# The first head's queries and keys projected together while x arrives, its values around the rows' norm

## The chip, the cores and the metric

The kernel runs on one core of a Trainium2 chip. A core has a matrix engine (TensorE, "PE" in the profile; its weight loads are "PEld"), three engines that work on tiles (VectorE "DVE", ScalarE "ACT", GpSimd "POOL"), and SyncE "SP", which here issues all transfers; sixteen DMA engines carry them. Each engine runs its own list of instructions in order and waits on semaphores for the others. The metric is the device time of one execution in microseconds; less is better.

## The reference

One layer of a streaming encoder is computed for 16 meta tokens, a prompt of 512 frames and 64 frames of a running stream, in fp32. Cut to what matters here:

```python
h = rmsnorm(x, norm_attn_g)              # x: (L, 2048)
z = h @ w_in                             # (2048, 3904): q | k | v of 8 heads, 128 columns each,
                                         # then latent queries, latent keys/values, rotary key
qd, kd, vd = z[..., :1024], z[..., 1024:2048], z[..., 2048:3072]
s = qd . kd * DIFF_SCALE + rel_bias[t5_bucket(kpos - qpos)]     # per head, two halves of 64
p = softmax(s[0]) - lam * softmax(s[1])
o_d = rmsnorm(p @ vd, diff_subln_g) * (1 - lam_init)
# a second head group on the latents, output projection, residual, SwiGLU FFN, final norm
```

`rmsnorm` divides each row by the root of its mean square. The new keys and values of each head are outputs too.

## The kernel before, in words

All 592 tokens (64 sample, 16 meta, 512 prompt) are held transposed: D = 2048 lies in 16 slices of 128 partitions (`KC` = 16), tokens along the free dimension, in two halves of 296 (`TH`). For accuracy each fp32 operand is split into a high and a low part (`split`, L155 to L157: ACT makes the high part at L156, DVE the low part at L153), and a product is three matmuls, high by high, high by low, low by high (`mm3`), for each half of the tokens: six matmuls for a slice. A projection (`project`) of 128 output columns takes 16 slices; its weights come in two halves of 8 slices (`weights`), each one transfer of 512 KB, split in one piece.

*The start.* x is loaded token by token into tiles `xn`, six row tiles (`tok`) for each quarter of D (`load_x`). `transpose_x` turns one slice into PSUM (L112) and has ACT and DVE write `xh` and `xl`, scaled by the norm's gain (`split_scaled`, L160 and L161), and DVE copy the slice to `xt` (L377, L382), which is stored to DRAM as `xspill` for the residual. Even slices use one pair of PSUM banks (`pxt`), odd slices two single ones (`pxa`, `pxb`). When the last slice of a quarter has been transposed, ACT squares its six row tiles with a running sum (L387) into `ssp`, and, since `xn` has two buffers per row tile, the quarter after next is loaded. The projection of head 0's queries runs along: slice kc is projected while slice kc + 1 is transposed.

The division by the norm is put off: `xh` and `xl` carry no norm, and the projected rows are multiplied by `rb`, the reciprocal root of each token's mean square in all partitions. It is made after the 16 slices: `ss` (L426, L427), `rsqrt`, six products with the identity (`prb`, L108 through the helper) and a copy (L434). Then comes the relative bias: `ptr` is the product of the bias table with a one-hot matrix, copied to `trs` (L446), stored to DRAM, spread over 128 rows (`tsk`, L449) and read back skewed as `bias` by each head.

*After the start* a planner (`Streams`) writes out the order of PE's work: `projections` goes through the heads (queries, keys, values, and then the latents), and each head's attention (`diff_attend`) takes PE between its slices, by rank. The planner counts PE's time and gives PSUM banks back after fixed delays (`st.give`). PE's instructions stay in the order in which the program names them; on the other engines the instructions are put in order when the program is built, by when their operands are expected.

PSUM has eight banks: two pairs for projections (`pjt`), one pair `sp` for scores and `pxt`, one single bank `tp`, one single bank `po`.

Of the kernel before, what the change touches and what calls it, by code (L numbers as in the profile page):

```python
# [19 lines left out]
P = 128  # L20
D = 2048
KC = D // P
# [93 lines left out]
def encoder_step(  # L116
# [19 lines left out]
    def load(dst, src):  # L136
        nc.sync.dma_start(dst, src)
# [155 lines left out]
    def ev(ps, n=TH):  # L293
        return ps[:, :, 0:n]
# [19 lines left out]
    with ExitStack() as ph:  # L314
# [7 lines left out]
        def pjt():  # L322
            return pj.tile([P, 2, 512], F32, name="ps", tag="ps")
# [4 lines left out]
        def tbank(name="tp"):  # L328
            return pst.tile([P, 512], F32, name=name, tag="tp")
# [11 lines left out]


        tok = [(0, OWN), (OWN, P), (208, 88), (TH, P), (424, P), (552, 40)]
        ps0 = pjt()
        with tc.tile_pool(name="xn", bufs=1) as xn:
            ssp = az.tile([P, 6, 4], F32, name="ssp")
            V.memset(ssp, 1.0)
            junk = xn.tile([P, 512], F32, name="junk")
            xt_in = {}

            def load_x(cg):
                cs = slice(cg * 512, (cg + 1) * 512)
                for j, (o, n) in enumerate(tok):
                    t = xn.tile([P, 512], F32, name="xn", tag=f"xn{j}", bufs=2)
                    if j == 0:
                        load(t[0:NS, :], x_sample[:, cs])
                        load(t[NS:OWN, :], meta[:, cs])
                    else:
                        load(t[0:n, :], x_prompt[o - OWN:o - OWN + n, cs])
                    xt_in[cg, j] = t  # L360

            def transpose_x(kc):
                cg, k = kc // 4, kc % 4
                if kc % 2 == 0:
                    sp = sbig("pxt")
                    banks = [sp[:, 0, 0:TH], sp[:, 1, 0:TH]]
                else:
                    banks = [tbank("pxa")[:, 0:TH], pso.tile([P, 512], F32, name="pxb", tag="po")[:, 0:TH]]
                for j, (o, n) in enumerate(tok):
                    b = o // TH  # L370
                    PE.transpose(banks[b][:, o - b * TH:o - b * TH + n],
                                 xt_in[cg, j][0:n, k * P:(k + 1) * P], ident[0:n, 0:n])
                xt = ztile("xt")
                g = gA[:, kc:kc + 1]
                if kc % 2 == 0:
                    split_scaled(hv(xh[kc]), hv(xl[kc]), ev(sp), g)
                    V.tensor_copy(hv(xt), ev(sp))  # L377
                else:
                    for b in range(2):
                        c = slice(b * TH, (b + 1) * TH)  # L380
                        split_scaled(xh[kc][:, c], xl[kc][:, c], banks[b], g)
                        V.tensor_copy(xt[:, c], banks[b])  # L382
                for o, n, c in KEPT:
                    store(xspill[kc, :, c:c + n], xt[:, o:o + n])
                if k == 3:
                    for j, (o, n) in enumerate(tok):
                        S.activation(junk[0:n], xt_in[cg, j][0:n], AF.Square, accum_out=ssp[0:n, j, cg:cg + 1])  # L387
                    if cg + 2 < 4:
                        load_x(cg + 2)

            load_x(0)
            gains = xn.tile([P, P], F32, name="gains")
            V.memset(gains, 0.0)
            rows = 0
            for g in (g_attn, g_ffn, g_fin, g_q, g_kv, g_sub):
                n = g.shape[0] // P
                load(gains[rows:rows + n, :], g.rearrange("(c p) -> c p", p=P))
                rows += n
            load_x(1)
            pg = tbank("pg")  # L400
            PE.transpose(pg[:, 0:P], gains, ident)
            gT = cp.tile([P, rows], F32, name="gT")
            V.tensor_copy(gT, pg[:, 0:rows])
            gA, gF, gE, gq, gkv, g08 = (gT[:, a:b] for a, b in ((0, 16), (16, 32), (32, 48), (48, 52), (52, 54), (54, 55)))
            first = project(ps0, w_in[:, 0:P], xs1)
            transpose_x(0)
            for kc in range(KC):
                if kc + 1 < KC:
                    transpose_x(kc + 1)
                next(first)  # L410

        ap = ph.enter_context(tc.tile_pool(name="ap", bufs=1))
# [13 lines left out]
        V.reduce_sum(ss, ssp, axis=AX.X)  # L426
        V.tensor_scalar(ss, ss, 1.0 / D, EPS, op0=ALU.mult, op1=ALU.add)  # L427
        rsqrt(rc, ss)
        pb = sbig("prb")
        for j, (o, n) in enumerate(tok):  # L430
            b = o // TH
            PE.matmul(pb[:, b, o - b * TH:o - b * TH + n], rc[0:n, j:j + 1].to_broadcast([n, P]),
                      ident[0:n, 0:n], start=True, stop=True)
        V.tensor_copy(hv(rb), ev(pb))  # L434

        with tc.tile_pool(name="xc", bufs=1, side="right") as xc:

            oh = xc.tile([32, NREL], F32, name="oh")
            load(oh, c_onehot)
            rbt = xc.tile([32, H], F32, name="rbt")  # L440
            load(rbt, rel_bias)
            ptr = sbig("ptr")
            trs = xc.tile([H, NREL], F32, name="trs")
            for i, (a, b) in enumerate(((0, 512), (512, NREL))):
                PE.matmul(ptr[0:H, i, 0:b - a], rbt, oh[:, a:b], start=True, stop=True)
                V.tensor_copy(trs[:, a:b], ptr[0:H, i, 0:b - a])  # L446
            store(trow, trs)
            for h in range(H):
                nc.sync.dma_start(tsk[h], trow[h:h + 1, :].to_broadcast([P, NREL]))  # L449

            lamt = xc.tile([P, 4, DH], F32, name="lamt")
            load(lamt, lam_p.rearrange("a b -> (a b)").unsqueeze(0).to_broadcast([P, 4 * DH]).rearrange(
                "p (a b) -> p a b", a=4))
            lprod = xc.tile([P, 2, DH], F32, name="lprod")
            lsum = xc.tile([P, 2], F32, name="lsum")
            V.tensor_tensor(lprod, lamt[:, 0:4:2, :], lamt[:, 1:4:2, :], op=ALU.mult)
            V.reduce_sum(lsum, lprod, axis=AX.X)
            S.activation(lsum, lsum, AF.Exp)
            V.memset(lamv[:, 0:1], 1.0)
            V.tensor_tensor(lamv[:, 1:2], lsum[:, 0:1], lsum[:, 1:2], op=ALU.subtract)  # L460
            V.tensor_scalar(lamv[:, 1:2], lamv[:, 1:2], LAM_INIT, None, op0=ALU.add)
            V.tensor_scalar(g08, g08, 1.0 - LAM_INIT, None, op0=ALU.mult)
# [113 lines left out]

        def projections():
            for h in range(H):
                ps = ps0 if h == 0 else pjt()
                if h:  # L580
                    yield from project(ps, w_in[:, h * P:(h + 1) * P], xs1)
                if h >= 2:
                    yield [scored[h - 2]]
                z = ztile()
                V.scalar_tensor_tensor(hv(z), ev(ps), DH ** -0.5, hv(rb), op0=ALU.mult, op1=ALU.mult)
                for c in range(2):
                    r = slice(c * DH, (c + 1) * DH)
                    split(qs[h % 2][c][0][r, :], qs[h % 2][c][1][r, :], z[r, :])

                ps = pjt()  # L590
                yield from project(ps, w_in[:, OFF_K + h * P:OFF_K + (h + 1) * P], xs1)
                if h >= 1:
                    yield [nat[2 * h - 1], nat[2 * h - 2]]
                z = ztile()
                V.tensor_tensor(hv(z), ev(ps), hv(rb), op=ALU.mult)
                kh = ap.tile([P, TP], F32R, name="kh", bufs=2)
                kl = ap.tile([P, TP], F32R, name="kl", bufs=2)
                split(kh[:, 0:T], kl[:, 0:T], z)
                nat[2 * h] = st.spawn(0, keys(h, z, kh, kl))

                ps = pjt()
                yield from project(ps, w_in[:, OFF_V + h * P:OFF_V + (h + 1) * P], xs1)
                if h >= 2:
                    yield [att[h - 2]]
                z = ztile()
                V.tensor_tensor(hv(z), ev(ps), hv(rb), op=ALU.mult)
                vh = ap.tile([P, 6, P], F32R, name="vh", bufs=2)
                vl = ap.tile([P, 6, P], F32R, name="vl", bufs=2)
                nat[2 * h + 1] = st.spawn(0, values(h, z, vh, vl))
                att[h] = st.spawn(1, diff_attend(h, kh, kl, vh, vl),  # L610
                                  [nat[2 * h], nat[2 * h + 1]] + ([att[h - 1]] if h else []))
# [5 lines left out]
                zs[i] = zl.tile([P, T], F32, name=f"zl{i}")  # L617
                V.tensor_tensor(hv(zs[i]), ev(ps), hv(rb), op=ALU.mult)

        for name in ("sp", "tp", "po"):  # L620
            st.bank(name, 1)
        st.spawn(9, projections())
        st.run()

# [794 lines left out]
```

## Time and profile before

| | |
|---|---|
| time, median of 3 runs | 2583.15 us (2583.13 to 2589.03) |
| the profiled execution's own time | 2593.06 us |
| its span in the profile | 2590.9 us |
| mean granted TensorE clock | 0.983 |
| PE busy | 2464.9 us, 95% |
| DVE, ACT, POOL busy | 71%, 41%, 29% |
| DMA | 307.73 MB, mean 119 GB/s |

The profile is of one execution. A page gives busy times, a picture of the span in 40 slices, the costliest groups of instructions with the idle time before them and what ended it. A row of the timeline has start, duration, engine, line, operation, written tile <- read tiles, and in brackets the idle time before it with its releaser. A row of the waits has who waited for whom: total, times, longest. A row of the windows has the stretch and its length, then busy time of PE, PEld, DVE, ACT, POOL with instruction counts, granted clock, DMA share, GB/s.

### The profile page before, as it was taken

To read this page: it belongs to the slowest core of one execution; us is meant where nothing else is said; L and a number is where in the kernel's file an instruction comes from. 1 tells how busy PE (TensorE), PEld (TensorE's weight loads), DVE (VectorE), ACT (ScalarE), POOL (GpSimd) and SP (SyncE) were. 2 spreads that over 40 slices of the span, in tenths; PEclk is the share of its full clock that TensorE was granted. 3 is DMA by queue.
4 is the path that set the end of the run, shared out by engine and by line. 5 is a ranking of instruction groups with operands and counts; after the bars stand their busy time and mean duration, and the time that the engine had idled before them with its cause. 6 is when DMAs were issued, how large, how long until landed. Compare 5 with 4: busy or idle time off the path is not lost. (4 is left out here: it accounts for less than half of the span.)

```text
span 2590.9 us, 44881 instructions
## 1 busy us (share of the span) xinstructions
PE 2464.9 (95%) x17847; PEld 2399.3 (93%) x17847; DVE 1837.4 (71%) x2955; ACT 1056.5 (41%) x1879; POOL 763.5 (29%) x614
## 2 busy tenths in 40 slices
PE   6999999989999999999999999999999899999997
PEld 5999999988999888999999999999999899999996
DVE  5455555556565568777677787777778899899874
ACT  5234333334443444333333333333334344444444
POOL 0000000000000265545545455464543221221244
PEclk9999999999999899999999999999999899999998
DMA  6433233334331553333333333333335543443334
GB/s 197 126 93 93 80 86 86 81 104 121 99 99 58 170 152 124 106 113 121 130 116 108 111 122 128 116 128 108 109 126 177 189 146 98 146 146 101 98 107 130
DMA packets 330563, 307.73 MB, mean 119 GB/s; under 512 B 24707, under 2 KB 298506, under 8 KB 330354
## 3 DMA queue, kind: packets, MB, share of 16 engines
q1 hardware_dynamic: 330354, 304.87, 37.7%
q8 instruction: 140, 2.29, 0.4%
q14 instruction: 69, 0.57, 0.1%
HBM read 250.82 MB, written 56.68 MB: 119 GB/s over the span
## 5 line engine op out<-in xcount | busy, mean ns | idle before, releaser
L1051 PE MATMUL m<-bh,wh 128*128 128x288 f32 x3584 | 971.8, 296 | 8.3 <-ACT wh L156 6.3
L1051 PE MATMUL m<-bl,wh 128*128 128x288 f32 x3584 | 970.4, 295 | 0.0
L1051 PEld LDWEIGHTS m<-bh,wh 128*128 128x128 f32 x3584 | 676.3, 189 | 10.7 <-ACT wh L156 8.2
L1051 PEld LDWEIGHTS m<-bl,wh 128*128 128x128 f32 x3584 | 680.0, 190 | 0.1
L1055 PE MATMUL m<-bh,wl 128*128 128x288 f32 x3584 | 589.3, 300 | 38.1 <-DVE wl L153 35.9
L1020 POOL TENSOR_TENSOR ws<-raw 128x512 f32<-128x512 f32 x256 | 359.3, 1412 | 765.1 <-DVE wl L153 533.6
L1055 PEld LDWEIGHTS m<-bh,wl 128*128 128x128 f32 x3584 | 512.2, 189 | 57.1 <-DVE wl L153 56.4
L156 ACT ACTIVATE wh<-ws 128x512 fp32r<-128x512 f32 (+1 forms) x340 | 288.3, 848 | 475.9 <-PE m L1051 339.2
L153 DVE TENSOR_TENSOR wl<-ws,wh 128x512 fp32r<-128x512 f32 (+1 forms) x340 | 377.5, 1115 | 56.7 <-ACT wh L156 52.7
L153 DVE TENSOR_TENSOR wl<-raw,wh 128x512 fp32r<-128x512 f32 x416 | 401.2, 985 | 14.3 <-ACT wh L156 14.1
L156 ACT ACTIVATE wh<-raw 128x512 fp32r<-128x512 f32 x416 | 248.0, 625 | 339.6 <-PE m L1051 297.6
L108 PE MATMUL ps<-xh,wh 128*128 128x296 f32 x992 | 228.9, 312 | 6.9 <-ACT wh L156 6.9
L108 PE MATMUL ps<-xl,wh 128*128 128x296 f32 x992 | 218.3, 302 | 0.0
L108 PE MATMUL ps<-xh,wl 128*128 128x296 f32 x992 | 218.1, 301 | 0.0
L108 PEld LDWEIGHTS ps<-xh,wh 128*128 128x128 f32 x992 | 163.1, 192 | 11.1 <-ACT wh L156 7.0
L108 PEld LDWEIGHTS ps<-xl,wh 128*128 128x128 f32 x992 | 163.5, 191 | 0.0
L108 PEld LDWEIGHTS ps<-xh,wl 128*128 128x128 f32 x992 | 163.1, 191 | 0.3 <-DVE wl L153 0.3
L1020 DVE TENSOR_TENSOR ws<-ws,raw 128x512 f32<-128x512 f32 x128 | 94.0, 737 | 97.6 <-POOL ws L1020 92.5
L153 DVE TENSOR_TENSOR wl<-wr,wh 128x1024 fp32r<-128x1024 f32 (+1 forms) x110 | 117.7, 1070 | 45.3 <-ACT wh L156 36.4
L1272 DVE TENSOR_TENSOR y<-y,m 128x288 f32<-128x288 f32 x280 | 125.4, 448 | 21.5 <-PE m L1055 20.3
L156 ACT ACTIVATE wh<-wr 128x1024 fp32r<-128x1024 f32 (+1 forms) x110 | 101.8, 929 | 80.5 <-PE ps L108 72.2
L518 POOL MEMSET bias<- 64x64 f32 x8 | 1.4, 170 | 409.7 <-DMA bias<-tsk 247.8
(361 smaller groups left out, 3426.7 us busy)
## 6 DMA issues: line engine op xcount, KB each, us to landing
raw<-in_ffn_w_gate SPq DMA_DIRECT2D x44, 1024.0 KB, 7.7
raw<-in_ffn_w_up SPq DMA_DIRECT2D x44, 1024.0 KB, 6.3
raw<-in_ffn_w_down SPq DMA_DIRECT2D x40, 1024.0 KB, 5.4
wr<-in_w_in SPq DMA_DIRECT2D x60, 512.0 KB, 4.0
actspill<-c SPq DMA_DIRECT2D x44, 288.0 KB, 2.2
sumspill<-c SPq DMA_DIRECT2D x20, 576.0 KB, 3.0
bl<-sumspill SPq DMA_DIRECT2D x80, 144.0 KB, 3.4
bl<-actspill SPq DMA_DIRECT2D x68, 144.0 KB, 4.1
```

Of the source, the lines that this page charges most:

```text
L108: self.tc.keep_in_program_order(self.pe.matmul(out, lhsT, rhs, start=start, stop=stop))
L153: V.tensor_tensor(lo, src, f32(hi), op=ALU.subtract)
L156: S.activation(hi, src, AF.Copy)
L518: G.memset(bias[0:64, 464:528], -BIG)
L1020: engine.tensor_tensor(w[:, k:k + m, :], pick(xs), pick(ys), op=op)
L1051: PE.matmul(banks[p], wh[:, k, :], x, start=first and new and k == 0 and x is hi, stop=False, skip_group_check=not new)
L1055: PE.matmul(banks[p], wl[:, k, :], hi, start=False, stop=last and k == n - 1, skip_group_check=not new)
L1272: V.tensor_tensor(c, c, banks[p], op=ALU.add)
```

## The change

- x's row tiles have four buffers, so no load of x waits for a transposition; the loads of the gains move ahead of x, and those of the first weights stand between the quarters of x.
- Head 0's queries and keys are projected in the same loop, slice by slice, into the two pairs of banks of `pjt`; the keys' weights have buffers of their own in the pool `xn` (`first_weights`).
- Head 0's values are projected after that loop into the pair `sp` (`psv`): the first 8 slices before the norm's products `prb`, the other 8 after them. `prb` and `ptr` move to the single banks; `ptr`'s two pieces use the one bank `tp` in turn.
- In `projections`, head 0 only takes the finished banks; the planner starts with the bank `sp` taken and gets it back when the values are read.

```diff
-        ps0 = pjt()
+        psq, psk, psv = pjt(), pjt(), None
         with tc.tile_pool(name="xn", bufs=1) as xn:
+            gains = xn.tile([P, P], F32, name="gains")
+            V.memset(gains, 0.0)
+            rows = 0
+            for g in (g_attn, g_ffn, g_fin, g_q, g_kv, g_sub):
+                n = g.shape[0] // P
+                load(gains[rows:rows + n, :], g.rearrange("(c p) -> c p", p=P))
+                rows += n
...
-                    t = xn.tile([P, 512], F32, name="xn", tag=f"xn{j}", bufs=2)
+                    t = xn.tile([P, 512], F32, name="xn", tag=f"xn{j}", bufs=4)
...
                         S.activation(junk[0:n], xt_in[cg, j][0:n], AF.Square, accum_out=ssp[0:n, j, cg:cg + 1])
-                    if cg + 2 < 4:
-                        load_x(cg + 2)
+
+            def first_weights(hf):
+
+                r = slice(hf * 8 * P, (hf + 1) * 8 * P)
+                return [weights(w_in[r, c:c + P].rearrange("(k p) c -> p k c", p=P), 8, P, pool=pool)
+                        for c, pool in ((0, wp), (OFF_K, xn))]
 
             load_x(0)
-            gains = xn.tile([P, P], F32, name="gains")
...
+            ws = first_weights(0)
             load_x(1)
+            load_x(2)
+            ws = [ws, first_weights(1)]
+            load_x(3)
...
-            first = project(ps0, w_in[:, 0:P], xs1)
             transpose_x(0)
             for kc in range(KC):
                 if kc + 1 < KC:
                     transpose_x(kc + 1)
+                for ps, (wh, wl) in zip((psq, psk), ws[kc // 8]):
+                    mm3([ps[:, 0, 0:TH], ps[:, 1, 0:TH]], wh[:, kc % 8, :], wl[:, kc % 8, :],
+                        halves(xh[kc]), halves(xl[kc]), kc == 0, kc == KC - 1)
+            psv = sbig("psv")
+            first = project(psv, w_in[:, OFF_V:OFF_V + P], xs1)
+            for _ in range(8):
                 next(first)
...
-        pb = sbig("prb")
+        pb = [tbank("prb"), pso.tile([P, 512], F32, name="prb", tag="po")]
         for j, (o, n) in enumerate(tok):
             b = o // TH
-            PE.matmul(pb[:, b, o - b * TH:o - b * TH + n], rc[0:n, j:j + 1].to_broadcast([n, P]),
+            PE.matmul(pb[b][:, o - b * TH:o - b * TH + n], rc[0:n, j:j + 1].to_broadcast([n, P]),
                       ident[0:n, 0:n], start=True, stop=True)
-        V.tensor_copy(hv(rb), ev(pb))
+        for b in range(2):
+            V.tensor_copy(rb[:, b * TH:(b + 1) * TH], pb[b][:, 0:TH])
+        for _ in first:
+            pass
...
-            ptr = sbig("ptr")
             trs = xc.tile([H, NREL], F32, name="trs")
-            for i, (a, b) in enumerate(((0, 512), (512, NREL))):
-                PE.matmul(ptr[0:H, i, 0:b - a], rbt, oh[:, a:b], start=True, stop=True)
-                V.tensor_copy(trs[:, a:b], ptr[0:H, i, 0:b - a])
+            for a, b in ((0, 512), (512, NREL)):
+                ptr = tbank("ptr")
+                PE.matmul(ptr[0:H, 0:b - a], rbt, oh[:, a:b], start=True, stop=True)
+                V.tensor_copy(trs[:, a:b], ptr[0:H, 0:b - a])
...
-                ps = ps0 if h == 0 else pjt()
+                ps = psq if h == 0 else pjt()
...
-                ps = pjt()
-                yield from project(ps, w_in[:, OFF_K + h * P:OFF_K + (h + 1) * P], xs1)
+                ps = pjt() if h else psk
+                if h:
+                    yield from project(ps, w_in[:, OFF_K + h * P:OFF_K + (h + 1) * P], xs1)
...
-                ps = pjt()
-                yield from project(ps, w_in[:, OFF_V + h * P:OFF_V + (h + 1) * P], xs1)
+                ps = pjt() if h else psv
+                if h:
+                    yield from project(ps, w_in[:, OFF_V + h * P:OFF_V + (h + 1) * P], xs1)
...
                 V.tensor_tensor(hv(z), ev(ps), hv(rb), op=ALU.mult)
+                if h == 0:
+                    st.give("sp", 1.5)
...
-        for name in ("sp", "tp", "po"):
-            st.bank(name, 1)
+        for name, n in (("sp", 0), ("tp", 1), ("po", 1)):
+            st.bank(name, n)
```

More of the change, by code (lines that the diff above doesn't have):

```diff
@@ L387, in transpose_x @@
                         S.activation(junk[0:n], xt_in[cg, j][0:n], AF.Square, accum_out=ssp[0:n, j, cg:cg + 1])
-                    if cg + 2 < 4:
-                        load_x(cg + 2)
+            def first_weights(hf):
+                r = slice(hf * 8 * P, (hf + 1) * 8 * P)
+                return [weights(w_in[r, c:c + P].rearrange("(k p) c -> p k c", p=P), 8, P, pool=pool)
+                        for c, pool in ((0, wp), (OFF_K, xn))]
             load_x(0)
-            gains = xn.tile([P, P], F32, name="gains")
[L393 to L398, printed above, removed]
+            ws = first_weights(0)
             load_x(1)
+            load_x(2)
+            ws = [ws, first_weights(1)]
+            load_x(3)
             pg = tbank("pg")
```

## The prediction

> **What bounds the kernel now.** I read the page's busy times and slices first, then PE's waits in the first 110 us, then stages by window, then the order of time around them.
>
> ```profile
> span 2590.9 us, 44881 instructions
> PE 2464.9 (95%) x17847; PEld 2399.3 (93%) x17847; DVE 1837.4 (71%) x2955; ACT 1056.5 (41%) x1879; POOL 763.5 (29%) x614
> ...
> PE   6999999989999999999999999999999899999997
> ```
> ```profile
> PE pg L112 <- DMA gains<-in_diff_subln_g: 10.0, 1, 10.0
> PE ps L108 <- ACT wh L156: 6.9, 1, 6.9
> PE pxa L112 <- DVE xt L382: 4.8, 2, 2.8
> ```
> ```profile
> 19.80:29.60 9.80, 9.74 (x38) 8.18 (x39) 4.44 (x7) 3.23 (x6) 0.00 (x0) 1.00 0.59 175
> 37.10:39.80 2.70, 0.00 (x0) 0.01 (x1) 1.75 (x5) 2.70 (x7) 0.00 (x0) 1.00 0.22 49
> 39.80:42.90 3.10, 3.07 (x13) 2.67 (x14) 2.54 (x6) 1.31 (x3) 0.00 (x0) 0.50 0.61 143
> ...
> 51.40:56.80 5.40, 5.40 (x22) 4.56 (x23) 3.47 (x8) 1.80 (x4) 0.00 (x0) 0.50 0.82 244
> ...
> 60.40:70.40 10.00, 8.29 (x35) 6.47 (x36) 5.50 (x8) 1.96 (x4) 2.56 (x8) 0.67 0.59 159
> 70.40:95.00 24.60, 24.60 (x183) 24.58 (x182) 6.39 (x8) 4.97 (x8) 0.14 (x1) 1.00 0.67 204
> ```
> ```profile
> 100.00:150.00 50.00, 50.00 (x375) 49.52 (x374) 26.46 (x60) 18.14 (x38) 0.14 (x1) 1.00 0.33 90
> ...
> 250.00:300.00 50.00, 50.00 (x371) 49.08 (x370) 27.98 (x61) 20.09 (x43) 0.15 (x1) 1.00 0.33 91
> ```
>
> PE fills the span except in the first slice, where the change is: 10 us before anything arrives, 6.9 for the first weights, 4.8 behind the copies of transposed x. After idling PE also runs at half rate: the granted clock (third number from the end of a row) is 0.50 for 3.1 us after an idle 2.7, and for 5.4 us later. From 19.8 to 29.6 the column says 1.00, but the counts give it away: 38 matmul records in 9.8 us, against 183 in 24.6. From 70 to 300 us PE is never idle, and the built instruction orders of both kernels are the same on every engine from about head 3's attention on. So what the start gains or loses passes straight to the end.
>
> **The change, part by part.** The sum is a race to one point: the first head's q, k and v projected, the norm broadcast (prb) and the bias row (ptr) done. All PE work up to there is the same in both.
>
> ```profile
> 30.94 0.54 PE L108 MATMUL ps<-xh,wh 128*128 128x296 f32 x2
> ...
> 32.63 0.54 PE L108 MATMUL ps<-xh,wh 128*128 128x296 f32 x2
> ...
> 71.19 0.44 PE L108 MATMUL ps<-xh,wh 128*128 128x296 f32 x2
> ...
> 72.01 0.44 PE L108 MATMUL ps<-xh,wh 128*128 128x296 f32 x2
> ...
> 84.31 0.60 PE L112 MATMUL pna<-ident,z 128*128 128x128 f32 x4
> ...
> 95.02 0.77 DVE L606 TENSOR_TENSOR z<-ps,rb 128x592 f32<-128x592 f32 x1 [2.30 <-PE ps L108]
> ```
>
> At full clock one slice of 128 rows of D costs 32.63 - 30.94 = 1.69 us with its transposes and 72.01 - 71.19 = 0.82 without, so 0.86 for the transposes. Before, PE ends v at about 94.8 (the copy follows at 95.02); some 0.75 us of that are transposes of the keys (pna and two smaller ones) which the changed kernel does later. The mark before is 94.1.
>
> (1) *The gains are loaded before x.* Six small loads now stand ahead of x on SP.
>
> ```profile
> 1.21 0.58 SPq L137 DMA_DIRECT2D xn<-in_x_sample  x1
> ...
> 4.74 0.33 SPq L137 DMA_DIRECT2D gains<-in_norm_attn_g  x1
> ...
> 8.10 0.22 SPq L137 DMA_DIRECT2D gains<-in_diff_subln_g  x1
> ```
> ```profile
> 8.00:9.00 1.00, 0.00 (x0) 0.00 (x0) 0.00 (x0) 0.97 (x4) 0.00 (x0) 1.00 0.11 29
> ```
> ```profile
> 14.00:21.00 7.00, 1.14 (x4) 1.00 (x4) 2.72 (x5) 4.67 (x11) 0.00 (x0) 1.00 1.04 317
> ```
>
> They took 3.6 us of SP with their waits, some 2.2 without. I take 2.5 (bounds 0 and 3.6). The first quarter of x, landed at 8.1 before (traffic falls to 29 GB/s), lands at 10.6. The transposes, which waited for the gains until 10.0, now wait for x: about the same.
>
> (2) *The first weights of q and k come right after that quarter.* 1.05 MB at the 317 GB/s of the busiest stretch is 3.3 us: landed at 14. Then ACT's split, and the first matmul at 15.4 instead of 19.9. A gain of 4.5 if nothing later took it back.
>
> (3) *All of x has its own buffers*, so all 28 loads and four weight loads (7 MB) stand on SP ahead of the first store of xspill; at 317 GB/s that is 22 us from x's first issue at 3.7, ended at 26 at best; I take 30, as the first quarter, 1.2 MB from 1.21 to 8.1, came slower. The copies xt have three buffers, so the fourth waits for the first store. What is late next is not this, however, but (4).
>
> (4) *ACT's queue.* Loaded early, x lets its squares be placed early. In the built order ACT runs all 24 squares and all four weight splits before the transposed slice 5 (xh), and DVE does the sum of the squares (ss) before the copy xt of slice 3. Engines run their queues in order, so PE's transposes of slice 5, which need that copy's bank, wait for the last square. This wait exists before too, at 50 us:
>
> ```profile
> 7.53 0.63 ACT L387 ACTIVATE junk<-xn 88x512 f32<-88x512 f32 x1
> ...
> 8.29 0.63 ACT L387 ACTIVATE junk<-xn 128x512 f32<-128x512 f32 x1
> ...
> 10.33 0.19 ACT L387 ACTIVATION_READ_ACCUMULATOR junk<-xn 40x1 f32 x1
> ...
> 11.65 0.75 ACT L160 ACTIVATE xh<-pxt,gT 128x592 fp32r<-128x592 f32 x1 [1.14 <-PE pxt L112]
> ...
> 12.34 0.51 ACT L160 ACTIVATE xh<-pxa,gT 128x296 fp32r<-128x296 f32 x1
> ...
> 18.75 1.06 ACT L156 ACTIVATE wh<-wr 128x1024 fp32r<-128x1024 f32 x1 [0.39 <-DMA wr<-in_w_in]
> ...
> 50.49 0.18 DVE L426 TENSOR_REDUCE ss<-ssp 128x6 f32<-128x24 f32 x1 [2.24 <-ACT junk L387]
> ...
> 51.39 0.72 PE L112 MATMUL pxa<-ident,xn 80*128 80x80 f32 x3 [2.07 <-DVE xt L382]
> ```
>
> A square costs 0.76 with its read (8.29 - 7.53). The first six end at 10.5 before, now at 13.0. Behind them stand 18 squares (13.7), four splits (4.2) and the xh of slices 0 to 4 (3 of 0.75, 4 of 0.51: 4.3): 22.2 us, so 35.2 at the earliest. ACT also waits for PE's transposes of slices 2, 3, 4. PE starts at 15.4 at half rate; taking the 9.7 us that the half rate lasted from 19.9, it is full from 25.1. Slice 0 ends at 18.7 (the k weights are split by then), transposes of 2 at 20.2, slice 1 at 23.1, transposes of 3 at 24.7, slice 2 at 26.5, transposes of 4 at 27.4. ACT then has xh of 4 to 28.2, five squares to 32.0, two splits to 34.1, six squares to 38.7. The bound above is all at half rate, some 1.8 later: 40.5. After ss and the first copy PE goes on at 39.7, having stood since 29.0.
>
> (5) *The rest of the loop.* 11 slices of transposes (0.86) and 12 of twofold projection (1.65) are 29.2 us. After 10 us idle the half rate, 3.1 to 5.4 us in the rows, costs half of that, 2.1. The loop ends at 71.0.
>
> ```profile
> L161 DVE SCALAR_TENSOR_TENSOR xl<-pxt,gT,xh 128x592 fp32r<-128x592 f32 x8 | 6.7, 832 | 11.5 <-ACT xh L160 11.5
> ```
>
> DVE's two passes over a slice are at most 1.7 (xl 0.83, the copy no more), ACT's two halves 1.0, against PE's 2.5: neither binds, and stores of three slices earlier have long landed.
>
> (6) *The values around the norm.* 16 slices of 0.82 are 13.2; prb, of which 12 matmuls took 1.69 at half rate (its row stands below), is about 1.05 in all at full rate, between the halves. The norm row is long ready, so the old stop for it is gone. v ends at 85.2 (call it E).
>
> (7) *ptr now uses one bank twice.* Its second matmul waits for the copy trs of the first, which stands on DVE behind z of v and a weight split whose ACT half starts at E:
>
> ```profile
> 60.47 1.69 PE L108 MATMUL prb<-ident,rc 80*128 80x80 f32 x12 [0.64 <-DVE rc L169]
> ...
> 63.03 1.23 PE L108 MATMUL ptr<-oh,rbt 32*8 32x512 f32 x2 [0.87 <-DVE rb L434]
> ...
> 64.30 0.68 DVE L446 COPY trs<-ptr 8x512 f32<-8x512 f32 x1 [0.51 <-PE ptr L108]
> ...
> 66.04 0.30 SPq L140 DMA_DIRECT2D trow<-trs  x1
> ...
> 75.50 1.23 DVE L153 TENSOR_TENSOR wl<-wr,wh 128x1024 fp32r<-128x1024 f32 x1 [7.11 <-DMA tsk<-trow]
> ...
> 84.36 0.14 POOL L518 MEMSET bias<- 64x64 f32 x1 [21.32 <-DMA bias<-tsk]
> ```
>
> 1.1 for the split's ACT half, 1.2 for DVE's, 0.7 for trs: ptr is done at E + 3.5, PE having stood 2.5 us, after which half rate (3.1 to 5.4 us) costs 2.0; bounds 0 and 2.7. The mark is reached, in full-clock terms, at 85.2 + 3.5 + 2.0 = 90.7. Behind trs the bias goes out and back: 18.3 us before (66.0 to 84.4), so E + 22; head 0's first scores stand 23 slices behind ptr, at E + 24 or later. No stall.
>
> Sum: 94.1 - 90.7 = 3.4 us less. The profiled execution took 2593.06, 10 us above the median of the runs; taken off the median, 2583.15 - 3.4 = 2579.8: **2580 us**. With 35.2 for ACT and no half rate after ptr the gain is 9, with 40.5 and the long half rates 0.
>
> **A rule against the row.** The sum takes 9.7 us of half rate at the start and some after a stop of 2.5. The rows have 3.1 as well, so a rival is that the clock rises within about 3.4 us and stays up through ptr: PE full from 18.8, transposes of slice 4 at 24.6, the last square at 35.9, loop end 67.8, mark at 85.6: 8.5 us less, 2575. [...] The trace before disagrees at both ends: 9.7 us at the start, and a stop of 2.07 us that was followed by 5.4 us at 0.50.
>
> **Other rivals.** *The squares don't gate, the loads do:* PE goes on at 31 instead of 39.7, loop end 62, 12 us less, 2571. For it: ACT is only 41% busy over the span. Against: the queue's sum, 22.2 us, is in the order itself.
> *Slower, by the bias:* the eight tsk writes and the bias read share the queue with weights; DVE would hold everything behind the first scores, weight splits included. It must be over 2 us late to cost anything, and 13 us late to reach 2591 (2 + 3.4 + 7.7), a path of 31 us where 18.3 is measured.
> *The change does nothing:* k's projection only fills time that PE then idles at slice 5, and the mark stays at 94: 2583. That is the forecast's upper bound.
>
> **How the numbers follow.** Differences under 0.3% (7.7 us) count as no change. Forecast with its bounds, nothing gained included (2574 to 2583): 0.6, nearly all of it within. The clock rival at 2575, just over the line: 0.16. Loads gate, 2571: 0.08. Slower through the bias or another late wait: 0.16, a third of it under 2591. So faster 0.24, same 0.64, slower 0.12. The range reaches past 2571 for the unknown start of x, and to 2589 for a small late wait.
>
> **What would show it.** PE waiting about 10 us at the transposes of slice 5 (pxa behind xt), with ss just ahead and the squares solid on ACT to about 38; the loop's end near 71; 2.5 us at ptr. Wrong if that wait is under 5 us (faster), or if PE waits for the scores' evacuation near 110 us (slower).

## The result, and the profile after

The changed kernel takes 2594.32 us (median of 13 runs, 2586.67 to 2601.67), the kernel before beside it 2584.74 us (13 runs): a ratio of 1.0035, 95% interval [1.0026, 1.0044]. That is 9 us slower, where 2580 was forecast, 3 faster. The forecast range ended at 2589.

The profiled execution of the changed kernel took 2594.32 us, its median; that of the kernel before took 2593.06, 8 us above its own. So their spans (2590.9 and 2592.4) nearly agree, and the loss must be read by place. PE's waits of the changed kernel in the first 130 us (waiting instruction <- releaser: total, times, longest):

```profile
PE pxa L112 <- DVE xt L389: 9.8, 1, 9.8
PE pnb L112 <- DVE na L490: 7.5, 1, 7.5
PE pg L112 <- DMA gains<-in_diff_subln_g: 4.6, 1, 4.6
PE pxt L112 <- DMA xn<-in_x_prompt: 3.1, 4, 1.4
PE ptr L108 <- DVE trs L462: 1.8, 1, 1.8
PE pxt L112 <- DMA xn<-in_meta_tokens: 1.8, 1, 1.8
PE ps L108 <- ACT wh L156: 1.5, 1, 1.5
```

The first and the fifth row are the stops that were forecast, at slice 5 and at ptr. The second was not. Now the start by its milestones (timeline rows; a row holds two matmuls, x2):

```profile
15.17 0.86 PE L108 MATMUL ps<-xh,wh 128*128 128x296 f32 x2 [1.45 <-ACT wh L156]
...
21.22 0.43 PE L108 MATMUL ps<-xh,wl 128*128 128x296 f32 x2
...
37.26 0.72 PE L112 MATMUL pxa<-ident,xn 80*128 80x80 f32 x3 [9.80 <-DVE xt L389]
...
86.06 0.64 PE L108 MATMUL ptr<-oh,rbt 32*8 32x144 f32 x2 [1.82 <-DVE trs L462]
...
89.60 0.43 PE L108 MATMUL ps<-xh,wh 128*128 128x296 f32 x2
```

The projection begins at 15.17, at half rate (0.86 a pair, then 0.43) until 21.2. The second ptr is done at 86.6, with half rate until 89.3 (1.4 us of loss): in full-clock terms the mark of the prediction is reached at 88.0, against 94.1 before. Up to there the change gains 6 us in these two executions (others of the same start gain less, see a_na). After it:

```profile
91.07 0.69 DVE L490 COPY na<-pna 128x512 f32<-128x512 f32 x1 [4.03 <-PE pna L112]
92.46 0.69 DVE L153 TENSOR_TENSOR vl<-na,vh 128x512 fp32r<-128x512 f32 x1 [0.70 <-ACT vh L156]
...
102.99 0.69 DVE L490 COPY na<-pna 128x512 f32<-128x512 f32 x1 [5.30 <-DMA out<-na]
```
```profile
87.06 0.30 SPq L140 DMA_DIRECT2D trow<-trs  x1
89.14 5.13 SPq L465 DMA_DIRECT2D tsk<-trow  x8
94.36 0.59 SPq L140 DMA_DIRECT2D out<-na  x1
```
```profile
97.00:100.40 3.40, 0.00 (x0) 0.00 (x0) 0.69 (x1) 0.00 (x0) 0.00 (x0) 0.89 1.07 354
100.40:103.80 3.40, 0.00 (x0) 0.01 (x1) 0.69 (x1) 0.00 (x0) 0.14 (x1) 0.50 0.84 249
103.80:107.20 3.40, 3.37 (x14) 3.40 (x15) 0.00 (x0) 0.27 (x1) 0.00 (x0) 0.50 0.36 105
107.20:109.80 2.60, 2.60 (x12) 2.58 (x12) 0.29 (x1) 0.28 (x1) 0.00 (x0) 0.50 0.00 0
109.80:113.20 3.40, 3.40 (x27) 3.39 (x26) 0.80 (x3) 1.44 (x4) 0.00 (x0) 0.99 0.07 19
```

The first fence is DVE, the second SP's issues, the third windows (after the lengths: busy time of PE, PEld, DVE, ACT, POOL; last three: granted clock, DMA share, GB/s). `natural` turns the values of head 0 round into the tile na, stores it, then does the same with the keys. na has one buffer, so the second copy waits for the first store. That store is ready at 91.8, issued at 94.36 behind the eight tsk writes (8 x 328 KB), and landed 8.6 us after its issue, the DMA engines being full from 97.0 to 100.4 (share 1.07, 354 GB/s). PE's next transpose, pnb, needs the bank that the second copy frees: PE stands 7.5 us and then runs 6.0 us at 0.50, a loss of 3.0. The 6 us ahead have become 4.5 behind in these two executions.

Before, the last of the tsk writes was issued 12 us ahead of the first of these stores, and the next one, of the same tile, came 13 us later:

```profile
68.84 5.08 SPq L449 DMA_DIRECT2D tsk<-trow  x8
...
85.67 0.39 SPq L140 DMA_DIRECT2D out<-na  x1
...
98.63 0.39 SPq L140 DMA_DIRECT2D out<-na  x1
```

The rest of the lag lies in heads 0 to 7. The last norm of an attention head (pq) starts at 559.9 before and 569.9 after, the same work having been done:

```profile
L108 PE MATMUL pq<-sq,ones x32: 403/406/408, 163.5 to 559.9; 128*128 128x288 f32 x32
```
```profile
L108 PE MATMUL pq<-sq,ones x32: 403/406/408, 173.3 to 569.9; 128*128 128x288 f32 x32
```

10.0 us late there, of which 4.5 are explained. From 110 to 550 us PE waits 5.4 us in five places before (all at sp behind nm, a bank of scores that DVE has not read yet), and after:

```profile
PE sp L108 <- DVE nm L549: 7.1, 8, 1.6
PE tp L112 <- DVE pol L153: 0.6, 1, 0.6
```

2.3 us more. Twice such stops were also followed by 3.4 us at half clock, 1.7 of loss each; before, in that execution, none. That is 4.5 + 2.3 + 3.4 = 10.2 against 10.0. The last term belongs to this execution: a_early and a_tskpool below have the same stops and no such spell.

### The profile page after: what moved, and what is told of

It reads as the page before. It is cut to its first block, busy times and chain, and to the rows that moved or that the text cites. A ratio compares the mean times of both kernels' runs of the same rounds, so it can differ in the third digit from the quotient of the medians.

```text
span 2592.4 us, 44875 instructions
## 1 busy us (share of the span) xinstructions
PE 2460.2 (95%) x17847; PEld 2393.7 (92%) x17847; DVE 1842.4 (71%) x2956; ACT 1057.7 (41%) x1879; POOL 764.7 (29%) x614
## 5 line engine op out<-in xcount | busy, mean ns | idle before, releaser
L108 PE MATMUL ps<-xh,wh 128*128 128x296 f32 x960 | 223.5, 314 | 1.5 <-ACT wh L156 1.5
L108 PE MATMUL ps<-xl,wh 128*128 128x296 f32 x960 | 212.8, 303 | 0.0
L108 PE MATMUL ps<-xh,wl 128*128 128x296 f32 x960 | 212.0, 303 | 0.0
L1040 DVE TENSOR_TENSOR ws<-ws,raw 128x512 f32<-128x512 f32 x128 | 100.9, 795 | 87.9 <-POOL ws L1040 83.0
```

What stands on the lines that cost most here:

```text
L108: self.tc.keep_in_program_order(self.pe.matmul(out, lhsT, rhs, start=start, stop=stop))
L1040: engine.tensor_tensor(w[:, k:k + m, :], pick(xs), pick(ys), op=op)
```

## The experiments

Theory 1: the gain was lost where na's store stands behind the tsk writes. Theory 2: it was lost whatever na does, in the order of heads 0 to 3. All fourteen kernels in one table (stops in us; pq is the start of the last head's norm in the profiled execution; "slice 5" is the wait at pxa, "pnb" that behind na):

| kernel | median us | ratio to before | slice 5 | ptr | pnb | pq |
|---|---|---|---|---|---|---|
| before | 2584.7 to 2587.0 | 1 | 2.1 and 2.8 | 0.8, 0.9 | none | 559.9 |
| the change | 2594.32 | 1.0035 [1.0026, 1.0044] | 9.8 | 1.8 | 7.5 | 569.9 |
| a_na | 2586.82 | 1.0005 [0.9994, 1.0016] | 9.8 | 1.8 | none | 563.0 |
| a_early | 2585.61 | 0.9998 [0.9989, 1.0007] | 9.8 | none | 3.3 | 557.7 |
| a_tskpool | 2597.25 | 1.0033 [1.0022, 1.0044] | 9.8 | 1.8 | 7.7 | 568.1 |
| a_sq | 2592.63 | 1.0018 [1.0010, 1.0027] | 5.9 | 1.8 | 7.6 | 567.5 |
| a_st | 2585.72 | 0.9993 [0.9984, 1.0003] | none | 1.8 | 10.1 | 558.1 |
| a_b2 | 2592.13 | 1.0014 [1.0004, 1.0024] | 3.4 | 1.8 | 8.0 | 565.5 |
| a_all | 2585.37 | 0.9998 [0.9989, 1.0008] | 6.3 | none | none | 554.6 |
| a_two | 2578.29 | 0.9955 [0.9940, 0.9970] | none | none | 2.3 | 549.7 |
| a_three | 2578.55 | 0.9954 [0.9937, 0.9970] | none | none | none | 545.8 |
| a_all2 | 2573.89 | 0.9956 [0.9943, 0.9968] | none | none | none | 545.3 |
| a_all3 | 2602.57 | 1.0062 [1.0047, 1.0076] | none | none | none | 572.1 |
| b_give | 2616.92 | 1.0121 [1.0107, 1.0135] | 2.2 and 2.7 | 0.8, 0.9 | none | 593.8 |

(The kernel before had medians from 2584.7 to 2587.0 beside the others; compare by the ratios, 0.001 of which is 2.6 us. pq is of one execution each and holds the luck of its clock.) The expectations of a_na, a_early and a_tskpool call the first of the two naturals the keys'. In the built order it is the values'; the wait is the same.

**a_na: a buffer for the values' na.**

```diff
-            na = ap.tile([P, 4, P], F32, name="na", tag="na")
+            if own:   # values of head 0
+                na = ap.tile([P, TQ], F32, name="sq")[:, 0:SEQ].rearrange("p (j c) -> p j c", j=4)
+            else:
+                na = ap.tile([P, 4, P], F32, name="na", tag="na")
```

> The changed kernel, with one thing undone: the na copy of head 0's values has a buffer of its own (the one that sq takes much later), so it no longer waits for the store of the keys' na. Theory 1 (that store, which stands on SP behind the eight tsk writes, is where the gain went): PE's wait at pnb behind na, 7.5 us, is gone with about 3 us of half rate after it; about 10 us less than the changed kernel, 2584, which is the time of the kernel before or a few us under it, and pq of head 0 comes 10 us earlier than 173.3. Theory 2 (the loss is in the order of heads 0 to 3 whatever na does: the waits of the scores behind nm turn up later): pq of head 0 comes earlier by 10, but the time stays within 3 us of 2594.

The stop at pnb is gone, the copy follows its transposes at once:

```profile
94.61 0.69 DVE L493 COPY sq<-pna 128x512 f32<-128x512 f32 x1 [4.32 <-PE pna L112]
97.50 0.69 DVE L493 COPY na<-pna 128x512 f32<-128x512 f32 x1 [0.81 <-PE pna L112]
```

The ratio falls by 0.0030, 8 of the 9 us. Theory 1 holds, theory 2 in its strict form (within 3 us of 2594) falls. But nothing is gained over the kernel before. The start is that of the changed kernel, yet in this execution its half rate lasted 9.8 us instead of 6.0:

```profile
16.04 0.86 PE L108 MATMUL ps<-xh,wh 128*128 128x296 f32 x2 [1.45 <-ACT wh L156]
...
26.03 0.43 PE L108 MATMUL ps<-xl,wh 128*128 128x296 f32 x2
```

So the mark came at 91.6, 2.5 us ahead of the kernel before and not 6 (in a_tskpool, of the same start too, at 90.1). The stops in the heads are those of the changed kernel, 2.3 us more than before, and two spells of half clock took 3.4 again: 3.2 behind, as pq shows (563.0 against 559.9).

**a_early: the bias row ahead of the second half of v.**

```diff
-        for _ in first:
-            pass
         with tc.tile_pool(name="xc", bufs=1, side="right") as xc:
...
                 PE.matmul(ptr[0:H, 0:b - a], rbt, oh[:, a:b], start=True, stop=True)
                 V.tensor_copy(trs[:, a:b], ptr[0:H, 0:b - a])
+                for _ in range(2):
+                    next(first)
...
+            for _ in first:
+                pass
```

> The changed kernel with the bias row's block (ptr, trs, trow, tsk) moved ahead of the second half of v, its two ptr matmuls two slices of v apart; na keeps its single buffer. Theory 1: the tsk writes are out some 8 us earlier, the store of the keys' na finds the queue free, PE's wait at pnb falls from 7.5 us to under 2, and the 1.8 us stop at ptr with its 3 us of half rate goes too: 2580 to 2584. Theory 2 (buffer and queue are not what costs): only the stop at ptr goes, 2 to 5 us less, 2589 to 2592. If the weights' loads are then what stands behind the tsk writes, a new wait of PE behind wh appears in v or head 1.

With the writes of tsk out from 81.2, the stop at pnb is 3.3 us (under 2 was expected) and the one at ptr is gone: 0.0037 less than the changed kernel, 10 us, at the slow edge of what theory 1 gave. About 3 of these are the stop at ptr with its half rate (1.8 + 1.4). The buffer was not touched here: a buffer of its own takes the stop at pnb away, earlier writes more than halve it. It takes both, a single buffer and its store behind 2.7 MB.

**a_tskpool: the tsk writes issued by POOL.**

```diff
-                nc.sync.dma_start(tsk[h], trow[h:h + 1, :].to_broadcast([P, NREL]))
+                nc.gpsimd.dma_start(tsk[h], trow[h:h + 1, :].to_broadcast([P, NREL]))
```

> The changed kernel with the eight tsk writes issued by POOL instead of SP; nothing else. If the store of the keys' na was late because its issue stood behind those eight on SP (issue at 94.4, pna copied at 91.8), it is issued some 2 us earlier and PE's stop at pnb falls from 7.5 to about 5; if it was late because its data shares the DMA engines with 2.7 MB of tsk (landing 8.6 us after the issue), the stop stays above 5 whatever the issuer. If each issuer has its own queue and the engines take turns between queues, the stop falls under 3 and the time by 5 to 8 us, to about 2587.

SP, then POOL, then DVE:

```profile
93.86 0.39 SPq L140 DMA_DIRECT2D out<-na  x1
```
```profile
91.74 4.29 POOL L465 DMA_DIRECT2D tsk<-trow  x8 [16.14 <-DMA trow<-trs]
```
```profile
105.39 0.69 DVE L490 COPY na<-pna 128x512 f32<-128x512 f32 x1 [10.17 <-DMA out<-na]
```

Now the store is issued right behind its copy (93.14 to 93.83), about as the fifth of the eight writes is, and lands 11.5 us later, against 8.6 after the issue in the changed kernel. From copy to copy it is 12.3 there and 11.9 in the changed kernel, and the ratio is no better: the place in SP's order did not matter. What is left is the traffic of the tsk writes, as the DMA engines were full meanwhile (share 1.06, 403 GB/s):

```profile
98.00:100.00 2.00, 0.44 (x4) 0.20 (x2) 0.00 (x0) 0.50 (x1) 0.00 (x0) 1.00 1.06 403
```

The store, with no tsk write ahead of it on SP, still took 11.5 us to land, where the sixteen of its size took 3.1 (median) in the kernel before. That it shared the engines with these writes is read from this and was not tried apart.

**a_sq: the squares one or two to a slice, and a_st: the xspill stores issued by POOL.** Two single edits at slice 5:

```diff
-                if k == 3:
-                    for j, (o, n) in enumerate(tok):
-                        S.activation(junk[0:n], xt_in[cg, j][0:n], AF.Square, accum_out=ssp[0:n, j, cg:cg + 1])
+                for j, (o, n) in [*enumerate(tok)][SQ[k]:SQ[k + 1]]:   # SQ = (0, 2, 4, 5, 6)
+                    tc.keep_in_program_order(
+                        S.activation(junk[0:n], xt_in[cg, j][0:n], AF.Square, accum_out=ssp[0:n, j, cg:cg + 1]))
```
```diff
-                    store(xspill[kc, :, c:c + n], xt[:, o:o + n])
+                    nc.gpsimd.dma_start(xspill[kc, :, c:c + n], xt[:, o:o + n])
```

> The changed kernel with the 24 squares kept in program order on ACT, one or two of them in each slice, so that none stands ahead of the xh of a slice that is due. If the squares are what gates slice 5: PE's wait at pxa (9.8 us) and the half rate after it (4.2 us) go, the loop ends near 58 instead of 68.4; the na store is late behind the tsk writes as before, so PE still waits about 7.5 us at pnb; the time is 10 us less, 2584. If the loads of x gate slice 5, the wait only changes its name to a DMA, and less than 4 us are gained.

> The changed kernel with one thing moved: the xspill stores of the loop are issued by POOL instead of SP, where they stood behind all loads of x. Spreading the squares alone left a stop of 5.9 us at slice 5, whose copy xt waited for the first store of xspill. Theory 1 (that store is the gate, the squares only fill the time): PE's wait at pxa falls from 9.8 us to under 3, the loop ends 7 to 10 us earlier than 68.4; with the stop at pnb left as it is the time is about 2585 to 2588. Theory 2 (the squares gate by themselves): the wait stays above 7 and the time within 3 us of 2594. If POOL's issue of a store is slow, the copies xt wait for stores again, later in the loop.

With the squares spread, the stop only falls from 9.8 to 5.9 us, and another wait stands behind it. The copy xt of slice 3 in a_sq, and the same copy in the changed kernel behind the last square and the sum (ss):

```profile
35.71 0.47 DVE L390 COPY xt<-pxa 128x296 f32<-128x296 f32 x1 [1.62 <-DMA xspill<-xt]
```
```profile
35.60 0.63 ACT L394 ACTIVATE junk<-xn 40x512 f32<-40x512 f32 x1
```
```profile
36.36 0.18 DVE L439 TENSOR_REDUCE ss<-ssp 128x6 f32<-128x24 f32 x1 [2.97 <-ACT junk L394]
36.57 0.17 DVE L440 TENSOR_SCALAR ss<-ss 128x6 f32<-128x6 f32 x1
36.65 0.47 DVE L389 COPY xt<-pxa 128x296 f32<-128x296 f32 x1
```

Two gates about a microsecond apart, as far as two executions can be laid side by side: the squares (36.65) and the first store of xspill (35.71). xt has three buffers, so the fourth copy needs the first store landed, and the stores stand behind all loads of x. Their first issue in the changed kernel and in a_st:

```profile
29.51 9.96 SPq L140 DMA_DIRECT2D xspill<-xt  x10
```
```profile
15.43 1.25 POOL L391 DMA_DIRECT2D xspill<-xt  x2 [14.98 <-DVE xt L384]
```

The 10 us expected of a_sq were wrong: 0.0017 of the ratio is 4. In a_st the stop is gone altogether, without an edit to the squares: with the stores out early, the built order on ACT has 15 of the 24 squares ahead of xh of slice 5 instead of all. So the late stores are the root, through the copies that wait for them and, as the order suggests, through what is built around them; no run moves the one without the other. a_st takes 0.0042 less than the changed kernel, 11 us, as theory 1 had it, and its stop at pnb has even grown to 10.1.

**a_b2: the joint projection without the buffers.** x has two buffers, as before the change.

```diff
-                    t = xn.tile([P, 512], F32, name="xn", tag=f"xn{j}", bufs=4)
+                    t = xn.tile([P, 512], F32, name="xn", tag=f"xn{j}", bufs=2)
...
+                    if cg + 2 < 4:      # behind the squares of a quarter
+                        load_x(cg + 2)
+                    if cg == 0:
+                        ws[1:] = [first_weights(1)]
...
-            load_x(2)
-            ws = [ws, first_weights(1)]
-            load_x(3)
```

> The joint projection of q and k alone: x has two buffers as before the change, a quarter being loaded when the one two before it has been used, and the second half of the first weights after the third quarter. It tells which part of the change gains the 6 us ahead of head 0. If the early loads do, PE waits for x at the third and fourth quarter (pxt or pxa behind xn, 5 us or more) and pq of head 0 is later than 173.3, 2595 to 2600. If the joint projection does, since x's stores now get out between the loads, the 9.8 us stop at slice 5 goes, smaller waits for x take its place, and the time is 2586 to 2594. The stop at pnb behind na stays in both.

The ratio is 0.0021 lower than the change's, 5 us: the stores get out between the loads, the stop is 3.4 instead of 9.8, and PE waits for x nowhere after 13 us. Its mark comes at about 85, 9 us ahead of the kernel before, against 2.5 to 6 with the early loads. The joint projection is what gains; as built, the early loads cost.

**Together.** a_all is a_na, a_early and a_sq. a_all2 adds a_st's edit; a_three is a_all2 without a_sq's, a_two is a_three without a_na's.

> The changed kernel with the three edits together: own buffer for the na of head 0's values, bias block ahead of the second half of v, squares one or two to a slice. If the three costs are separate stops of PE on one path they add up: 10 (na), 3 to 5 (ptr), 10 (squares), so 2570, about 15 us under the kernel before. If the order in heads 0 to 3 gives part of it back (scores behind nm), 2575 to 2580.

> Own buffer for the na of head 0's values, bias block ahead of the second half of v, squares one or two to a slice, and the xspill stores issued by POOL. Against the kernel with the first three: the 6.3 us stop at slice 5 and 3 to 4 us of half rate after it go; pq of head 0 comes at about 150 (158.0 with the three edits); 2576 to 2579, and with the same 3 to 6 us given back in heads 0 to 7. If nothing that is gained ahead of head 0 reaches the end, 2585 again.

> Own buffer for the na of head 0's values, bias block ahead of the second half of v, xspill stores issued by POOL; the squares are left as the changed kernel has them. If the late stores were what put all squares ahead of slice 5 in ACT's order, this does as well as with the squares spread by hand: 2574, 0.4 to 0.5% under the kernel before. If the squares gate by themselves, 2579 to 2584.

> As the kernel before in this list, but na has its single buffer again. The tsk writes and the naturals both come 10 us earlier, so the second na copy waits for the first one's store as in the kernel with the early bias block alone, which stood 3.3 us there: a stop of 3 to 5 us at pnb, with 0 or 3.4 us at half rate, 4 to 7 us more than with the own buffer, 2578 to 2581. If the queue is free by then, no stop and no difference.

a_all2, a_three and a_two all take 0.9954 to 0.9956 of the kernel before, 11 to 12 us less (by the medians of so few runs, 8 to 13), and are the fastest kernels here; a_two needs only two of the edits. PE's waits of a_three from 13 to 130 us:

```profile
PE ps L108 <- ACT wh L156: 1.4, 1, 1.4
PE pxt L112 <- PE ps L108: 0.2, 1, 0.2
PE ps L108 <- DVE xl L161: 0.2, 1, 0.2
```

Spreading the squares adds nothing once the stores are out. The buffer adds nothing that the ratios can show, though 4 to 7 us were expected and a_two keeps a stop of 2.3 us. a_all was a miss: at pq it is 15 us ahead of the changed kernel, but its ratio shows 0.0037, 10 us, and equals the kernel before. The profiled executions take from 2021 to 2031 us from pq to the end, and that of a_all 2029; why its runs keep so little stays open.

**a_all3 and b_give: the stops in the heads.** a_all2 and the kernel before, with one number of the planner changed:

```diff
-                    st.give("sp", 1.2 + 0.0015 * W)
+                    st.give("sp", 2.0 + 0.0015 * W)
```

> The kernel before in this list, and the planner told that the scores' bank comes free 0.8 us later, so that it puts a projection slice between scores that now follow each other. The stops at sp behind nm in heads 0 to 7, 7.7 us in ten stops, with up to 3.4 us of half rate behind them, should go: 5 to 10 us less than with the four edits alone, 2568 to 2573. If those stops cost nothing that counts, no difference.

> The kernel before, with the scores' bank freed 0.8 us later in the planner and nothing else. Its stops at sp behind nm are 5.4 us in five places. If the same stops in the changed kernel (7.1 us, and two spells of half rate) are the part of the loss that na does not explain, the kernel before gains 4 to 6 us too, about 2580; if not, within 2 us of 2585.

Both expectations fell: 28 us slower than a_all2, 31 slower than before. Waiting longer for the bank does not put projections between the scores, it pushes more of the scores together: in the place below, from 257 to 265, five groups of scores follow each other with no projection between them. PE's waits of b_give from 110 to 560 us, and one such place (windows):

```profile
PE sp L108 <- DVE nm L533: 14.7, 18, 1.6
```
```profile
257.50:260.90 3.40, 1.76 (x11) 1.21 (x11) 3.36 (x9) 1.78 (x4) 0.00 (x0) 1.00 0.01 2
260.90:264.30 3.40, 1.86 (x12) 1.42 (x11) 2.10 (x9) 1.88 (x6) 0.00 (x0) 0.50 0.71 176
264.30:267.70 3.40, 3.40 (x17) 3.40 (x18) 2.82 (x6) 1.62 (x5) 0.14 (x1) 0.50 0.17 60
267.70:271.10 3.40, 3.40 (x28) 3.39 (x27) 1.34 (x5) 0.71 (x3) 0.00 (x0) 1.00 0.06 14
```

Four short stops, 3.2 us in two windows, and 6.8 us with half the clock from the second window on, in each of four heads: 9.3 us more of stops and 13.6 of lost clock, 23 of the 34 us by which pq is later; the rest was not traced. They show what such stops cost; that the 2.3 us by which the changed kernel's stops differ come from its other order in heads 0 to 3 is read from the traces and was not tried apart.

## Why the prediction was wrong

- **(1), (2) the start: right.** First projection forecast at 15.4, measured 15.17. The half rate from there lasted 6.0 us, not 9.7, but that was this execution's luck: of the twelve traces of the changed kernel and its variants, four show 5 to 6 us and eight 8.4 to 10.4.
- **(3) the stores: the first dismissal that failed.** "What is late next is not this, however, but (4)": a_sq shows the store gating a microsecond behind the squares, and a_st that it is the root.
- **(4) the stop at slice 5: right in place and size.** Forecast from 29.0 to 39.7, measured from 27.4 to 37.26, with the last square and ss just ahead, as written (the square ended at 36.3, not 38.7). The cause was only half of it.
- **(5), (6): right.** The loop ended at 68.3 for a forecast 71.0 and v at 83.1 for 85.2, since less half rate came at the start; in a_na and a_tskpool, of the same start, the loop ended at 71.8 and 70.4. prb took 1.55 us where 1.05 was counted.
- **(7) ptr: right.** 2.5 us and 2.0 of half rate were forecast, 1.8 and 1.4 measured. The mark came at 88.0 for a forecast 90.7, a gain of 6 for 3.4; with 91.6 and 90.1 in a_na and a_tskpool the forecast is in the middle. The bias was back at 103.6, within E + 22, and nobody waited for it.
- **The step that failed is the last of (7): "No stall."** It followed the bias's own path behind the tsk writes and asked who waits for the bias. It did not ask what else stands on the queue behind 2.7 MB: the store of the values' na, whose tile has one buffer and, q, k and v now being ready together, is wanted again 3 us later rather than 13 (transposes pna at 90.4 and 93.3). That took 7.5 + 3.0 us in the profiled execution, and a buffer of its own (a_na) takes 8 of the 9 us off. The rival "slower, by the bias" named the queue and the writes, with the wrong victim. Its 0.16 was to cover any other late wait too, but its path had to be 13 us late, and it was priced too low.
- **"What the start gains or loses passes straight to the end" failed as well.** The orders agree from about head 3 on, but heads 0 to 3 were reordered, 2.3 us of stops. Of the two spells of half clock, the one at 427.3 follows stops that the kernel before has too, without a spell: that one was chance.
- **The clock rival** failed at both ends: its 3.4 us is the length of a spell (39.82 to 43.23 in the kernel before), but no run shows full clock that soon after the first projection (the earliest came after 5 us), and the 1.8 us stop at ptr was followed by 3.4 us at half clock (85.99 to 89.40). Its mark of 85.6 was missed by 2.4 us or more.

## What to carry to other kernels

When a change makes several things ready at once, list every single-buffered tile whose next use comes closer and ask where in the DMA traffic the store that frees it stands; here the 2.7 MB written just ahead of it became a stop of 7.5 us on PE. Look at who waits behind a large transfer, not only at who waits for it. And do not stop at the first gate: take it away in thought and ask what ends last then, for here two were about a microsecond apart, and moving the root (stores issued behind all the loads) did away with both.

## What the runs showed of the hardware

**The half clock came on a grid of 3.41 us.** The spells of half clock are about 3.4, 6.8, 10.2 ... us long (3.413, 6.827, 10.240 in the clock records of the kernel before and the changed one; but for the last of a trace, cut short by its end), and in one trace they begin on one grid (in the changed kernel at 99.64, 318.10, 427.32: 64 and 32 times 3.413 apart). I laid that grid on the fourteen traces, took PE's idle share in each window that had the full clock, and counted how often the next window was at half (from 34 us on):

```
idle share of a window      windows   next one at half clock
under 0.25                     9714          0
0.25 to 0.40                    181          4
0.40 to 0.50                     71         14
0.50 to 0.60                     60         53
over 0.60                        85         85
```

So in these traces a window that was idle for half its length or more (1.7 us) was followed by one at half clock in 138 of 145 cases, one idle for less than a quarter in none of 9714. A longer stop that straddled an edge could pass: in the changed kernel 2.51 us, from 597.12 to 599.63 over the edge at 597.99, with the clock at 1.00 up to 604.8. The same two stops (0.81 and 0.92 us) of the changed kernel and of a_early, in windows of the grid:

```profile
423.89:427.30 3.41, 1.71 (x16) 1.38 (x14) 2.94 (x8) 2.48 (x4) 0.00 (x0) 1.00 0.12 38
427.30:430.71 3.41, 3.38 (x17) 3.38 (x18) 3.03 (x7) 1.43 (x4) 0.14 (x1) 0.50 0.71 199
```
```profile
412.94:416.35 3.41, 1.85 (x17) 1.52 (x15) 2.79 (x6) 2.37 (x4) 0.00 (x0) 1.00 0.09 11
416.35:419.76 3.41, 3.24 (x27) 3.24 (x28) 3.17 (x9) 1.40 (x5) 0.14 (x1) 1.00 0.76 212
```

Busy 1.71 of 3.41 was followed by a window at 0.50, a loss of 1.7 us; busy 1.85 by one at 1.00, the second stop reaching over the edge there. Where the grid lies differs from execution to execution (its first line stands 2.3 us after the span's start in the kernel before, 0.7 in the changed one), and the same start came to its mark at 88.0, 90.1 and 91.6 us (the changed kernel, a_tskpool, a_na). So two single profiles must not be compared by their spans. What ends the half rate at the start, after 5 us in one trace and 13 in another (b_give), the grid alone does not tell; that stays open.
